# Attention on one core: K's and V's rows dealt four in a row to a partition, in every chunk of every batch

## The chip, the cores and the metric

The kernel runs on one core of one Trainium2 chip. The metric is the device time in microseconds (us) of one execution. Beside the timed runs there is one profiled execution, from which all rows of the profile come.

The core's engines are TensorE (PE, with its weight loads shown apart as PEld), VectorE (DVE), ScalarE (ACT), GpSimd (POOL) and SyncE (SP). Transfers between HBM and SBUF run on 16 DMA engines, whichever engine issued them.

## The reference

Inputs q, k and v have the shape (8, 2048, 512) in fp32; all 8 batches are attended over separately, with one head of width 512.

```python
scores = np.matmul(q, k.transpose(0, 2, 1)) / np.sqrt(d_k)
attn_weights = special.softmax(scores, axis=-1).astype(np.float32)
return np.matmul(attn_weights, v)
```

A sum over the keys does not depend on their order, so any order of a batch's keys gives the same output, if K's rows and V's rows are dealt in the same order. The order of q's rows is that of the output's rows.

## The kernel before

**Layout.** A batch has 2048 rows of q, k and v: 16 blocks of 128 rows (`NKB`), or four chunks of four blocks (`CH = 4`). Rows lie on the 128 partitions. Before the change row n * 128 + p of a batch lies on partition p as block n, for q, k and v alike (`srcs`, from L118).

**Loads.** All loads of fp32 inputs into fp16 tiles are casting DMAs that POOL issues (`load`, L133, for k and q; `load_v`, L221, for v). One load takes a chunk: 128 partitions, four rows of 512 elements each. A row of HBM is 2 KB, and its fp16 copy 1 KB. k and q chunks go to `stage` tiles, of which there are two, shared by both; v goes straight to one of two `vraw` tiles (named vh in the profile), one for odd and one for even batches.

**Transposes.** k and q are needed with the width on the partitions. In batch 0 most of this is done by PE (`first_transpose`, `transposed`), and from batch 1 on by DMA transposes that SP issues (L160), two for each chunk, into `kraw` and `qraw`. POOL may issue a load into a stage tile only when the transposes of the chunk before it in that tile are done, and SP may issue a transpose only when the load has landed. SP also issues every store of the output (L474), in the same queue.

**Matmuls.** Both matrix products are done by Strassen's scheme with seven products of halves in place of eight: sums of blocks are made on DVE (`k_sums` L195 to L198, `q_sums` L212 to L215, `v_sums` L229 to L232, `p_sums` L396 to L399), and a second level of the scheme is used in the product with V (`vi_sums` L267 to L270, `a_sums` L603 to L606, `fine`, whose matmuls are L649). The matmuls of the scores are L343 (`Group.product`) and, for the parts without the scheme, L286 and L302; those of the product with V are L452 (`Pair.product`) and L649. V is the moving operand. Between the products ACT and DVE copy and add PSUM banks (L354 to L368, L664 to L677), ACT does the exponentials (L279), and ACT, DVE and POOL scale and add the output halves (L461, L464, L570; for some the DMA adds them, L565). There are eight tiles for output halves.

**The sum of the weights.** V's second block of a pair has a column of ones next to it, at element 512 of its row, so that one of the matmuls has 257 columns instead of 256 and yields the sum of the weights. POOL writes this column once for each of the two tiles (L855 and L787).

**Order.** The whole order is written out by hand. A batch is four groups of 28 slots; `PRODUCTS`, `SUMS` and `PLAN` say in which slot of which group a product, a sum, a load or a transpose is issued. `PLAN` (L765 to L777) issues the loads and transposes of the next batch. Each engine runs its instructions in that order, and waits where an input is not ready.

**The start.** Batch 0's first row blocks are loaded apart: n = 0 of q by SP and of k by ACT, without a cast (`load_first`, L140), and n = 1 to 3 of q and k by POOL in turn (L833), 128 runs each. Then come k's second chunk in two pieces, the other chunks of q and k, which go into tiles that are free until later (named right and left in the profile), and V. Before the second half of V's load, and before the loads of batch 1, POOL waits at small copies (`gate`, L887, L890, L891).

Of the kernel before, what the change touches and what calls it, by code (L numbers as in the profile page):

```python
# [12 lines left out]
def kernel(  # L13
# [21 lines left out]
    nc = tc.nc  # L35
    P = 128
    B, T, D = q.shape
    F16 = mybir.dt.float16
# [13 lines left out]
    NJ = NKB // 2  # L52
    CH = 4
    NCH = NKB // CH
    H = D // 2
    VP = D + 2
    TP = H + 2
    NG = NJ // 2
    NE = 6
# [9 lines left out]
    const = ctx.enter_context(tc.tile_pool(name="const", bufs=1))  # L69
# [32 lines left out]
    qraw = [const.tile([P, 2 * NT, ND, P], F16, name=f"qraw{n}") for n in range(2)]  # L102
    qsum = [const.tile([P, NT, 2, P], F16, name=f"qs{n}") for n in (1, 2, 4)]

    vraw = [const.tile([P, NJ, 2, VP], F16, name=f"vh{n}") for n in range(2)]
    vt1 = const.tile([P, NJ, TP], F16, name="vt1")
    vt2 = const.tile([P, NJ, H], F16, name="vt2")
    vt4 = const.tile([P, NJ, H], F16, name="vt4")
# [2 lines left out]
    if not ALL:  # L111
# [3 lines left out]
    staged = {}  # L115
    pts = {}

    srcs = {  # L118
        "k": k.rearrange("b (n p) d -> b p n d", p=P),
        "q": q.rearrange("b (n p) d -> b p n d", p=P),  # L120
        "v": v.rearrange("b (n p) d -> b p n d", p=P),
    }

    def load(what, b, c, pieces=(CH,), room=None):
        t = staged.get((what, b, c))
        if room is not None:
            t = staged[what, b, c] = room
        if t is None:
            t = staged[what, b, c] = stage.tile([P, CH, D], F16, tag="stage", name="stage")
        n = CH - sum(pieces)  # L130
        for w in pieces:
            at = c * CH + n
            nc.gpsimd.dma_start(out=t[:, n:n + w, :], in_=srcs[what][b, :, at:at + w, :])  # L133
            n += w

    firsts = {}

    def load_first(what, n, queue, room):
        firsts[what, n] = room
        queue.dma_start(out=room, in_=srcs[what][0, :, n, :])  # L140

    def first_transpose(what, n):

# [12 lines left out]
    def dma_transpose(what, b, c, h):  # L156
        src = staged.pop((what, b, c)) if h else staged[what, b, c]
        dst = raw_of(what, b, c)
        ns = slice(h * CH // 2, (h + 1) * CH // 2)
        nc.sync.dma_start_transpose(  # L160
            out=dst[:, ns].rearrange("p n c r -> p (n c) r"),
            in_=src[:, ns].rearrange("p n d -> p (n d)"),
        )
# [52 lines left out]
        ]  # L216

    def load_v(b, c):
        dst = vraw[b % 2][:].rearrange("p j s d -> p (j s) d")
        ns = slice(c * CH, (c + 1) * CH)  # L220
        nc.gpsimd.dma_start(out=dst[:, ns, 0:D], in_=srcs["v"][b, :, ns, :])  # L221

    def v_sums(b, c=None):
        vh = vraw[b % 2]
        js = slice(0, NJ) if c is None else slice(c * NI, (c + 1) * NI)
        b11, b12 = vh[:, js, 0, 0:H], vh[:, js, 0, H:D]
        b21, b22 = vh[:, js, 1, 0:H], vh[:, js, 1, H:D]
        return [
            lambda: sub(vt1[:, js, 0:H], b12, b11),  # L229
            lambda: sub(vt2[:, js], b22, vt1[:, js, 0:H]),  # L230
            lambda: sub(b12, b22, b12),
            lambda: sub(vt4[:, js], b21, vt2[:, js]),  # L232
        ]

    def vi_blocks(b):
        lo, hi = slice(0, NI), slice(NI, NJ)
        vh = vraw[b % 2][:].rearrange("p j s d -> p s j d")
        return vh[:, :, lo, 0:P], vh[:, :, lo, P:H], vh[:, :, hi, 0:P], vh[:, :, hi, P:H]

    def t3_inner(b, s):  # L240
# [70 lines left out]
    class Group:  # L311
# [6 lines left out]
        def product(self, n):  # L318
            c, j = divmod(self.j, 2)
            a11, a12, a21, a22 = k_blocks(c)  # L320
            b11, b12, b21, b22 = q_blocks(self.sp)
            _, s1, s2, s4 = kops[c]
            t1, t2, t4 = qsum
            t3 = t3_of(self.sp)
            if n == 1:
                if self.sp not in pts:
                    new_p(self.sp)
                self.left, self.right = pts[self.sp][0:2]
                self.x = bank("qx")
# [12 lines left out]
            for dc in range(2):  # L342
                nc.tensor.matmul(  # L343
                    dst[:], lhs[:, j, dc, :], rhs[:, :, dc, :],
                    start=(n in (1, 5) and dc == 0), stop=(dc == 1),
                    skip_group_check=True,
                )
            getattr(self, f"after{n}", lambda: None)()
# [66 lines left out]
    class Pair:  # L415
# [8 lines left out]
        def product(self, n, j0=0, j1=NJ):  # L424
            g = self.g
            left, right = pts[g // 2][0:2]
            s1, s2, s4 = (t[:, :, part(self.which)] for t in psums[g])
            vh, t1, t2, t4 = vraw[g // NQT % 2], vt1, vt2, vt4
            cols = columns(g, self.which)
            alone = g >= NP - 2 and self.which == "b"  # L430
            own = "q" if alone else "p"
            if n == 1 and j0 == 0:
                self.x = bank("px")
            elif n == 2 and type(self) is Pair:
                self.y = bank(own + "y")
            elif n == 5:
                self.z = bank(own + "z")
            lhs, rhs, dst = {
                1: (lambda j: left[0][:, j, cols], lambda j: vh[:, j, 0, 0:H], "x"),
                2: (lambda j: left[1][:, j, cols], lambda j: vh[:, j, 1, 0:width], "y"),  # L440
                3: (lambda j: s4[:, j, :], lambda j: vh[:, j, 1, H:D + 1], "z"),
                4: (lambda j: right[:, j, 1, cols], lambda j: t4[:, j, :], "x"),
                5: (lambda j: s1[:, j, :], lambda j: t1[:, j, 0:H + 1], "z"),
                6: (lambda j: s2[:, j, :], lambda j: t2[:, j, :], "x"),
                7: (lambda j: right[:, j, 0, cols], lambda j: vh[:, j, 0, H:D], "x"),
            }[n]
            dst = getattr(self, dst)
            width = H + 1 if n in (3, 5) or (n == 2 and g == 0) else H
            first = n in (1, 5) or (n == 2 and type(self) is Pair)
            last = n in (2, 3, 4)  # L450
            for j in range(j0, j1):
                nc.tensor.matmul(  # L452
                    dst[:, 0:width], lhs(j), rhs(j),
                    start=(first and j == 0), stop=(j == NJ - 1),
                    skip_group_check=True,
                )
            if j1 == NJ:
                getattr(self, f"after{n}", lambda: None)()
# [325 lines left out]
    def prefetch(g, slot):  # L784
        b, qt = divmod(g, NQT)
        if (g, slot) == (0, 12):
            nc.gpsimd.memset(vraw[1][:, :, 1, D:D + 1], 1.0)  # L787
# [42 lines left out]
        staged[what, 0, 0] = spool.tile([P, CH, D], F16, tag=f"s{n + 1}", name="first")  # L830
    for n in range(1, CH):
        for what in "qk":
            nc.gpsimd.dma_start(out=staged[what, 0, 0][:, n], in_=srcs[what][0, :, n, :])  # L833
    nc.vector.tensor_copy(out=ident[:], in_=ident32[:])
    new_p(0)
    new_p(1)
# [18 lines left out]
    nc.gpsimd.memset(vraw[0][:, :, 1, D:D + 1], 1.0)  # L855
    dummies = {name: bank(name) for name in ("qy", "qz")}

    def idle(n, name="qy", w=512):
# [29 lines left out]
    firsts.pop("v")()  # L888

    nc.gpsimd.tensor_copy(out=gate[:], in_=qraw[1][:, NT - 1, ND - 1, 0:1])  # L890
    nc.gpsimd.tensor_copy(out=gate[:], in_=vraw[0][:, NJ - 1, 1, D - 1:D])  # L891

    def step(n=1):
        for _ in range(min(n, len(background))):
# [22 lines left out]
    for slot in range(14):  # L917
        n, at = divmod(slot, len(QORDER))
        old, what = QORDER[at]
# [23 lines left out]
    for g in range(NP):  # L943
# [4 lines left out]
        for slot in range(NS + 6):  # L948
            n, at = divmod(slot, len(QORDER))
            old, what = QORDER[at]  # L950
# [3 lines left out]
            if slot < NS:  # L954
# [6 lines left out]
                right = prev if at == 2 else None  # L961
# [42 lines left out]
```

## Time and profile before

| | us |
|---|---|
| median of 3 timed runs | 787.62 |
| lowest and highest of them | 787.57, 787.89 |
| the profiled execution | 788.82 |
| span of the profiled execution, first to last instruction | 787.0 |

The granted TensorE clock is 1.000 in the whole span. Busy shares of the span: PE 99%, PEld 68%, DVE 90%, ACT 81%, POOL 15%; the packets of queue 0 (the loads that POOL issues) take 45.0% of the 16 DMA engines' time, those of queue 1 (SP's transposes and stores) 42.1%.

How to read the rows: a group of instructions is named by its line, engine, operation and tiles (out<-in), then come its count, busy time, the mean ns of one, and the idle time of its engine just before it with what ended it. A wait is "who <- what it waited for: total us, times, longest us". In a DMA queue's row stand packets, MB and the share of 16 engines' time. A row of stretches has the length and then the busy time of each engine, with the number of instructions.

### The profile page before, as it was taken

How to read it: one execution, taken by the hardware profiler on the slowest of the kernel's cores; microseconds unless marked ns; L12 is line 12 of the kernel's file. 1: busy time of each engine (PE TensorE's matmuls, PEld its weight loads, DVE VectorE, ACT ScalarE, POOL GpSimd, SP SyncE). 2: the span in 40 equal slices, each digit the busy share in tenths (PEclk: the TensorE clock that was granted, in tenths of full speed). 3: DMA queues.
4: the chain of work that ended last, by engine and by line, in shares of the span. 5: the costliest groups of instructions: out<-in, count | busy, mean ns of one | idle time of the engine just before them, and what ended most of it. 6: DMA issues, size and time to landing. Idle time of an engine off the chain costs nothing.

```text
span 787.0 us, 18104 instructions
## 1 busy us (share of the span) xinstructions
PE 780.7 (99%) x6570; PEld 536.2 (68%) x6570; DVE 711.7 (90%) x1583; ACT 638.4 (81%) x1322; POOL 115.3 (15%) x157
## 2 busy tenths in 40 slices
PE   9999999999999999999999999999999999999998
PEld 6567666666666666666766666676666666666686
DVE  4799999989999899998999989999899998999864
ACT  4688888888888888888888888888888888888852
POOL 5011102012021020211102121021210212100000
PEclk9999999999999999999999999999999999999999
DMA  9999993999839999499976999579993999912122
GB/s 188 170 155 168 172 171 72 193 186 193 163 59 198 147 169 188 89 188 192 185 120 117 186 184 175 110 142 191 168 208 62 160 179 193 192 49 62 47 68 95
DMA packets 210298, 117.13 MB, mean 149 GB/s; under 512 B 126368, under 2 KB 209952, under 8 KB 210208
## 3 DMA queue, kind: packets, MB, share of 16 engines
q0 software_dynamic: 52528, 51.91, 45.0%
q1 hardware_dynamic: 157392, 63.73, 42.1%
q8 instruction: 51, 0.84, 0.4%
q14 instruction: 39, 0.32, 0.1%
q10 hardware_dynamic: 288, 0.33, 0.1%
HBM read 100.73 MB, written 33.55 MB: 171 GB/s over the span
## 4 chain that ended last, share of the span: by engine, by line
PE 94%; DMA 3%; ACT 1%; issue 1%; DVE 1%; POOL 0%; DVEq 0%; ACTq 0%; POOLq 0%
PE t L343 45%; PE t L452 29%; PE t L649 17%; PE t L286 2%; DMA out_dram<-o 2%; PE tr L170 1%; DMA first<-in_q_dram 1%; PE t L302 0%; POOL first L833 0%; ACT o L461 0%; ACT cz L359 0%; POOL o L570 0%; ACT t L354 0%; DVE s L397 0%; ACT left L279 0%
## 5 line engine op out<-in xcount | busy, mean ns | idle before, releaser
L461 ACT ACTIVATE o<-t,r 128x256 f32<-128x256 f32 x300 | 136.7, 478 | 75.8 <-DVE r L487 28.6
L343 PE MATMUL t<-qraw,kraw 128*128 128x512 f16 x728 | 198.1, 379 | 0.1
L279 ACT ACTIVATE left<-t 128x512 f16<-128x512 f32 (+1 forms) x260 | 154.0, 599 | 17.3 <-PE t L343 7.3
L343 PE MATMUL t<-qs,ks 128*128 128x512 f16 x488 | 138.8, 379 | 0.7 <-ACT t L354 0.7
L279 ACT ACTIVATE right<-cz 128x1024 f16<-128x1024 f32 x122 | 129.7, 1063 | 2.3 <-DVE cz L365 2.2
L343 PEld LDWEIGHTS <-kraw 128*128 128x128 f16 x976 | 87.0, 97 | 57.9 <-issue 0.6
L452 PEld LDWEIGHTS <-right 128*128 128x128 f16 x1024 | 99.4, 98 | 37.0 <-DVE right L398 1.4
L452 PEld LDWEIGHTS <-s 128*128 128x128 f16 x1072 | 102.1, 97 | 29.9 <-issue 0.3
L649 PEld LDWEIGHTS <-si 128*128 128x128 f16 x1044 | 76.2, 97 | 36.6
L359 ACT COPY cz<-t 128x512 f32<-128x512 f32 x120 | 70.3, 585 | 35.5 <-PE t L343 34.1
L343 PEld LDWEIGHTS <-ks 128*128 128x128 f16 x732 | 67.9, 97 | 41.4 <-issue 1.4
L368 DVE TENSOR_TENSOR cz<-t,cz 128x512 f32<-128x512 f32 x122 | 83.6, 685 | 11.8 <-ACT o L461 7.0
L464 DVE SCALAR_TENSOR_TENSOR o<-t,r,o 128x256 f32<-128x256 f32 x148 | 69.3, 478 | 19.8 <-ACT ci L667 7.5
L365 DVE TENSOR_TENSOR cz<-t,cz 128x512 f32<-128x512 f32 x122 | 83.3, 683 | 3.8 <-PE t L343 3.3
L649 PEld LDWEIGHTS <-left 128*128 128x128 f16 x928 | 66.1, 97 | 20.7
L354 ACT COPY t<-t 128x512 f32<-128x512 f32 x120 | 69.7, 581 | 4.7 <-PE t L343 1.1
L343 PE MATMUL t<-qraw,ks 128*128 128x512 f16 x244 | 72.5, 378 | 0.2 <-ACT cz L359 0.2
L452 PE MATMUL t<-vt,s 128*128 128x256 f16 (+1 forms) x560 | 72.5, 273 | 0.0
L343 PE MATMUL t<-qs,kraw 128*128 128x512 f16 x244 | 72.5, 379 | 0.0
L362 ACT COPY cz<-t 128x512 f32<-128x512 f32 x122 | 70.9, 581 | 0.4
L649 PE MATMUL t<-vh,left 128*128 128x128 f16 x696 | 67.4, 219 | 0.0
L452 PE MATMUL t<-vh,s 128*128 128x257 f16 x512 | 67.0, 273 | 0.1
(104 smaller groups left out, 1208.0 us busy)
## 6 DMA issues: line engine op xcount, KB each, us to landing
out_dram<-o SPq DMA_DIRECT2D x256, 128.0 KB, 3.7
vh<-in_v_dram POOLq DMA_DIRECT2D x32, 512.0 KB, 9.1
stage<-in_q_dram POOLq DMA_DIRECT2D x28, 512.0 KB, 7.0
stage<-in_k_dram POOLq DMA_DIRECT2D x28, 512.0 KB, 8.2
o<-o POOLq DMA_DIRECT2D x14, 128.0 KB, 2.7
right<-in_q_dram POOLq DMA_DIRECT2D x2, 512.0 KB, 10.5
right<-in_k_dram POOLq DMA_DIRECT2D x2, 512.0 KB, 12.8
qraw<-stage SPq DMA_TRANSPOSE x56, 6.2
```

The source lines that it names most:

```text
L279: nc.scalar.activation(out=out_, in_=in_, func=EXP, scale=inv_sqrt_d)
L286: nc.tensor.matmul(st[:], kops[c][0][:, n, dc, :], qraw[0][:, half * NT:(half + 1) * NT, dc, :], start=(dc == 0), stop=(dc == ND - 1),)
L343: nc.tensor.matmul(dst[:], lhs[:, j, dc, :], rhs[:, :, dc, :], start=(n in (1, 5) and dc == 0), stop=(dc == 1), skip_group_check=True,)
L354: f(out=self.y[:], in_=self.x[:])
L359: f(out=self.cz[:, 1, :], in_=self.z[:])
L362: nc.scalar.copy(out=self.cz[:, 0, :], in_=self.x[:])
L365: nc.vector.tensor_add(self.cz[:, 1, :], self.x[:], self.cz[:, 1, :])
L368: nc.vector.tensor_add(self.cz[:, 0, :], self.z[:], self.cz[:, 0, :])
L452: nc.tensor.matmul(dst[:, 0:width], lhs(j), rhs(j), start=(first and j == 0), stop=(j == NJ - 1), skip_group_check=True,)
L461: nc.scalar.activation(out=out_, in_=src, func=COPY, scale=r[:])
L464: nc.vector.scalar_tensor_tensor(out=out_, in0=src, scalar=r[:], in1=out_, op0=MULT, op1=ADD)
L649: nc.tensor.matmul(dst, lhs[:, j, :], rhs[:, j, :], start=(n == 1 and j == 0), stop=(j == NI - 1), skip_group_check=True,)
```

## The change

The rows of k and v are dealt so that, within each chunk of 512 rows, partition p holds the rows 4 p to 4 p + 3, which are adjacent in HBM. q's rows keep their order, with the chunk as an index of its own. A k load's run grows from one row to four (8 KB read, 4 KB written), where a whole chunk is loaded; k's second chunk in batch 0, loaded in two pieces, gets runs of two rows, and k's first four blocks in batch 0 keep runs of one row, 8 KB apart.

For v, the column of ones had stood after each row (a row took 514 elements, the column filled only for the second of a pair). It now stands after each pair (a pair takes 1026 elements), so that the two rows of a pair are adjacent and a v load's run grows to two rows (4 KB read, 2 KB written). All reads of v are written for the new layout.

```diff
-    VP = D + 2
+    VP = 2 * D + 2
...
-    vraw = [const.tile([P, NJ, 2, VP], F16, name=f"vh{n}") for n in range(2)]
+    vraw = [const.tile([P, NJ, VP], F16, name=f"vh{n}") for n in range(2)]
...
-        "k": k.rearrange("b (n p) d -> b p n d", p=P),
-        "q": q.rearrange("b (n p) d -> b p n d", p=P),
-        "v": v.rearrange("b (n p) d -> b p n d", p=P),
+        "q": q.rearrange("b (c n p) d -> b c p n d", p=P, n=CH),
+        "k": k.rearrange("b (c p n) d -> b c p n d", p=P, n=CH),
+        "v": v.rearrange("b (c p n) d -> b c p n d", p=P, n=CH),
...
-            at = c * CH + n
-            nc.gpsimd.dma_start(out=t[:, n:n + w, :], in_=srcs[what][b, :, at:at + w, :])
+            nc.gpsimd.dma_start(out=t[:, n:n + w, :], in_=srcs[what][b, c][:, n:n + w, :])
...
-        queue.dma_start(out=room, in_=srcs[what][0, :, n, :])
+        queue.dma_start(out=room, in_=srcs[what][0, 0][:, n, :])
...
-        dst = vraw[b % 2][:].rearrange("p j s d -> p (j s) d")
-        ns = slice(c * CH, (c + 1) * CH)
-        nc.gpsimd.dma_start(out=dst[:, ns, 0:D], in_=srcs["v"][b, :, ns, :])
+        js = slice(c * CH // 2, (c + 1) * CH // 2)
+        src = srcs["v"][b, c].rearrange("p (j s) d -> p j (s d)", s=2)
+        nc.gpsimd.dma_start(out=vraw[b % 2][:, js, 0:2 * D], in_=src)
+
+    def v_of(b):
+        return vraw[b % 2][:, :, 0:2 * D].rearrange("p j (s d) -> p j s d", s=2)
+
+    def ones_of(n):
+        return vraw[n][:, :, 2 * D:2 * D + 1]
...
-                1: (lambda j: left[0][:, j, cols], lambda j: vh[:, j, 0, 0:H], "x"),
-                2: (lambda j: left[1][:, j, cols], lambda j: vh[:, j, 1, 0:width], "y"),
-                3: (lambda j: s4[:, j, :], lambda j: vh[:, j, 1, H:D + 1], "z"),
+                1: (lambda j: left[0][:, j, cols], lambda j: vh[:, j, 0:H], "x"),
+                2: (lambda j: left[1][:, j, cols], lambda j: vh[:, j, D:D + width], "y"),
+                3: (lambda j: s4[:, j, :], lambda j: vh[:, j, D + H:2 * D + 1], "z"),
...
-                7: (lambda j: right[:, j, 0, cols], lambda j: vh[:, j, 0, H:D], "x"),
+                7: (lambda j: right[:, j, 0, cols], lambda j: vh[:, j, H:D], "x"),
...
-            nc.gpsimd.dma_start(out=staged[what, 0, 0][:, n], in_=srcs[what][0, :, n, :])
+            nc.gpsimd.dma_start(out=staged[what, 0, 0][:, n], in_=srcs[what][0, 0][:, n, :])
```

`v_sums` and `vi_blocks` read V through `v_of`, the two memsets write the column through `ones_of`, and the last gate reads the last element of V in the new layout; these lines are left out.

More of the change, by code (lines that the diff above doesn't have):

```diff
@@ L218, in load_v @@
     def load_v(b, c):
-        dst = vraw[b % 2][:].rearrange("p j s d -> p (j s) d")
-        ns = slice(c * CH, (c + 1) * CH)
-        nc.gpsimd.dma_start(out=dst[:, ns, 0:D], in_=srcs["v"][b, :, ns, :])
+        js = slice(c * CH // 2, (c + 1) * CH // 2)
[5 more added lines that the diff above has]
+        return vraw[n][:, :, 2 * D:2 * D + 1]
     def v_sums(b, c=None):
-        vh = vraw[b % 2]
+        vh = v_of(b)
         js = slice(0, NJ) if c is None else slice(c * NI, (c + 1) * NI)
@@ L236, in vi_blocks @@
         lo, hi = slice(0, NI), slice(NI, NJ)
-        vh = vraw[b % 2][:].rearrange("p j s d -> p s j d")
+        vh = v_of(b).rearrange("p j s d -> p s j d")
         return vh[:, :, lo, 0:P], vh[:, :, lo, P:H], vh[:, :, hi, 0:P], vh[:, :, hi, P:H]
@@ L786, in prefetch @@
         if (g, slot) == (0, 12):
-            nc.gpsimd.memset(vraw[1][:, :, 1, D:D + 1], 1.0)
+            nc.gpsimd.memset(ones_of(1), 1.0)
         for kind, what, c, *h in PLAN.get((qt, slot), ()):
@@ L854 @@
     nc.gpsimd.memset(ui[1][:, :, P:P + 1], 1.0)
-    nc.gpsimd.memset(vraw[0][:, :, 1, D:D + 1], 1.0)
+    nc.gpsimd.memset(ones_of(0), 1.0)
     dummies = {name: bank(name) for name in ("qy", "qz")}
@@ L890 @@
     nc.gpsimd.tensor_copy(out=gate[:], in_=qraw[1][:, NT - 1, ND - 1, 0:1])
-    nc.gpsimd.tensor_copy(out=gate[:], in_=vraw[0][:, NJ - 1, 1, D - 1:D])
+    nc.gpsimd.tensor_copy(out=gate[:], in_=vraw[0][:, NJ - 1, 2 * D - 1:2 * D])
     def step(n=1):
```

## The prediction

> **What bounds the kernel now.** I read the busy line of the page first, then the stretches of the span, then the chain of waits at the start and round the one gap in the middle, then the waits of the engines and of the SP queue, and the DMA views last.
>
> ```profile
> PE 780.7 (99%) x6570; PEld 536.2 (68%) x6570; DVE 711.7 (90%) x1583; ACT 638.4 (81%) x1322; POOL 115.3 (15%) x157
> ...
> 0.00:24.00 24.00, 22.37 (x168) 14.44 (x169) 11.16 (x24) 11.87 (x22) 10.43 (x22) 1.00 1.10 191
> 24.00:287.00 263.00, 262.59 (x2166) 176.56 (x2165) 246.52 (x543) 219.05 (x448) 39.34 (x54) 1.00 0.97 156
> 287.00:300.00 13.00, 12.42 (x108) 8.42 (x106) 11.08 (x29) 10.42 (x24) 2.22 (x3) 1.00 1.26 198
> 300.00:768.00 468.00, 468.00 (x4004) 323.80 (x4002) 434.89 (x974) 392.37 (x820) 63.30 (x78) 1.00 0.83 144
> 768.00:787.04 19.04, 15.29 (x136) 12.96 (x134) 8.04 (x16) 4.73 (x10) 0.00 (x0) 1.00 0.28 92
> ```
>
> The stretch rows give the length, then the busy time of PE, PEld, DVE, ACT and POOL, the granted clock, the DMA share and GB/s. From 300 to 768 us PE has no idle time at all (468.00 of 468.00) while the DMA engines carry 0.83. The whole budget of PE idle time is 24.00 - 22.37 = 1.63 us at the start, 0.41 up to 287, 0.58 in the 13 us after it, none to 768, and 19.04 - 15.29 = 3.75 at the end: 6.4 us. A busy PE in this view is not PE at its peak, but a load can only shorten time in which PE waits for it, so this budget is the most that faster loads could touch.
>
> Who waits for a transfer?
>
> ```profile
> POOL stage L133 <- DMA qraw<-stage: 186.0, 14, 16.3
> ...
> POOL gate L891 <- DMA vh<-in_v_dram: 6.8, 1, 6.8
> ...
> ACT o L461 <- DMA out_dram<-o: 1.2, 2, 0.9
> ...
> DVE ks L195 <- DMA kraw<-stage: 1.1, 1, 1.1
> ...
> PEld L170 <- DMA first<-in_q_dram: 0.4, 1, 0.4
> ...
> SPq L160 <- DMA stage<-in_q_dram: 68.2, 14, 19.8
> ...
> SPq L160 <- DMA stage<-in_k_dram: 3.3, 2, 2.9
> ```
>
> Columns: total us, times, longest. The large waits belong to POOL (it waits for a stage buffer before it may issue the next load) and to SP (it waits for a q load before it may transpose it). Neither reaches PE: ACT, DVE and PE wait for stores, transposes and first rows for 1.2 + 1.1 + 0.4 = 2.7 us in the whole run, and none of them waits for a V load; POOL's gate at the start does, for 6.8 us, and holds only the loads of the next batch.
>
> **The change part by part.**
>
> *The K and V loads in steady state (32 chunks each).* A chunk goes on moving 1 MB of fp32 into 512 KB of fp16; its runs grow from 2 KB to 8 KB (K) and 4 KB (V), so 512 runs become 128 and 256.
>
> ```profile
> DMA packets 2464, 2.46 MB, mean 205 GB/s; under 512 B 78, under 2 KB 2463, under 8 KB 2463
> ...
> q0 software_dynamic: 2463, 2.44, 123.1%
> ...
> q0 software_dynamic: 52528, 51.91, 45.0%
> ...
> q8 instruction: 51, 0.84, 0.4%
> ...
> vh<-in_v_dram POOLq DMA_DIRECT2D x32, 512.0 KB, 9.1
> ...
> stage<-in_k_dram POOLq DMA_DIRECT2D x28, 512.0 KB, 8.2
> ```
>
> The first two rows are from the stretch 12 to 24 us, where nearly only casting loads run. They land 205 GB/s of fp16, which is 410 GB/s of fp32 read, and a packet occupies its engine for 1.231 x 16 x 12 us / 2463 = 96 ns. A chunk of 1 MB therefore takes 1.05 MB / 410 GB/s = 2.6 us of pure transfer; the 8 to 9 us to landing are the issue, other traffic and the receipt. What would a packet of 8 KB read cost? No row shows one that casts. At the low end it costs less than four packets of 2 KB (4 x 96 = 384 ns) by whatever is fixed in a packet; were a quarter of the 96 ns fixed (an estimate), 4 KB packets would save an eighth and 8 KB packets 19%, 0.5 us of K's 2.6. At the high end stand the instruction fetches (16 KB each, 0.84 MB in 51): 0.4% x 16 x 787 us / 51 = 988 ns, 62 ns per KB where a 2 KB casting packet takes 48, so 29% more, +0.8 us a K chunk. I take a few per cent less, nearest to the casting rows. Either end is hidden: k transposes made DVE wait once (1.1 us) and V never, and PE stood still for none of it in the 468 us. Cost: 0.0. If the cover were gone, 28 later K chunks at +0.8 us could cost up to 22 us, but it would need each of them to be late already, and one in 28 is.
>
> *POOL's issue.*
>
> ```profile
> L221 POOL DMA_DIRECT2D vh<-in_v_dram x32 | 26.1, 815 | 0.8 <-PE t L649 0.5 <-DMA stage<-in_k_dram 0.3
> ...
> L133 POOL DMA_DIRECT2D stage<-in_k_dram x30 | 24.4, 815 | 103.9 <-DMA qraw<-stage 77.3 <-DMA kraw<-stage 14.7 <-ACT left L279 11.2
> ...
> L833 POOL DMA_DIRECT2D first<-in_k_dram x3 | 1.7, 575 | 0.0
> ```
>
> A load of 512 runs holds POOL 815 ns, one of 128 runs 575. So K's loads issue up to 0.24 us faster and V's by some 0.16 (256 runs, in between). POOL is busy 15% and waits 104 us ahead of these K issues alone; the saving is waiting in another place: 0.0.
>
> *V's new layout.* The tile changes from rows of 514 to pairs of 1026 elements; matmuls still stream 256 or 257 adjacent elements, and the sums keep their shapes.
>
> ```profile
> L229 DVE TENSOR_TENSOR vt<-vh x16: 671/679/685, 37.2 to 696.6; 128x1024 f16<-128x1024 f16 x16
> ...
> L232 DVE TENSOR_TENSOR vt<-vh,vt x16: 677/686/1022, 46.7 to 730.4; 128x1024 f16<-128x1024 f16 x16
> ...
> L213 DVE TENSOR_TENSOR qs<-qraw,qs 128x1024 f16<-128x1024 f16 x16 | 11.6, 725 | 0.1
> ...
> L452 PE MATMUL t<-vh,s 128*128 128x257 f16 x512 | 67.0, 273 | 0.1
> L452 PE MATMUL t<-vt,s 128*128 128x256 f16 x512 | 66.3, 273 | 0.0
> ```
>
> V's sums at an odd pitch (median 679 to 686 ns) take what Q's sums of the same size in an even layout take (725 mean), and the matmuls on vh and on vt are equal at 273. Pitch has no price in these rows, either way: 0.0.
>
> *The start.* K's first rows are now every fourth row of the chunk: 2 KB runs as before, 8 KB apart in HBM. q's order is unchanged.
>
> ```profile
> 1.25 2.29 POOL first L833 x4
> 3.54 5.07 DMA first<-in_q_dram
> 8.65 0.40 PE tr L170 x4
> ...
> 6.00:8.00 2.00, 1.76 (x22) 1.58 (x20) 1.15 (x3) 0.43 (x1) 2.00 (x4) 1.00 1.23 185
> 8.00:10.00 2.00, 1.80 (x25) 1.47 (x23) 1.14 (x4) 0.66 (x2) 2.00 (x4) 1.00 1.17 178
> ```
>
> The chain of waits: four small loads are issued, the fifth (q, n=3) lands 5.07 us after its own issue, and from 8.65 on the chain is PE. Before it in the same queue stand q and k for n=1 and n=2, all of 2 KB runs then as now. I take 0.0. Above, K's scattered rows could read slower (a rival below); below, if the larger runs behind them left these loads alone sooner, the 0.24 + 0.20 = 0.44 us that PE idles in 6 to 10 us is all there is.
>
> *The one gap in the middle.*
>
> ```profile
> 276.59 0.74 POOL L133 DMA_DIRECT2D stage<-in_k_dram  x1 [11.17 <-ACT left L279]
> ...
> 278.71 0.78 POOL L221 DMA_DIRECT2D vh<-in_v_dram  x1
> ...
> 278.80 12.35 DMA out_dram<-o
> ...
> 291.18 0.47 ACT L461 ACTIVATE o<-t,r 128x256 f32<-128x256 f32 x1 [0.91 <-DMA out_dram<-o]
> ...
> out_dram<-o SPq DMA_DIRECT2D x256, 128.0 KB, 3.7
> ```
>
> A store that usually lands in 3.7 us took 12.35 among a K and a V load issued beside it; ACT had no free output half, came 0.91 us late, and PE lost the 0.58 us of the stretch 287 to 300. Both loads beside it are of the changed kind. If they leave the engines a little earlier, this gap shrinks; it may as well turn up in another batch. I count half of it: -0.3 us (ends -0.58 and +0.58).
>
> **Sum:** 0 + 0 + 0 + 0 - 0.3 = -0.3 us. The profiled execution took 788.82 us with a span of 787.0 (1.8 outside it); its own time after would be 788.5. The three timed runs have the median 787.62, 1.2 below the profiled one; the difference carries over: **787.3 us**. A measurement of this kernel can tell about 0.2% (1.6 us) from no change, so the forecast is no change.
>
> **The rivals.**
>
> *Long packets hold up the stores: slower.* The SP queue's stores share the 16 engines with POOL's loads. If an engine finishes a packet before it turns to another queue, each of a store's 128 / 16 = 8 packets per engine can wait for a K packet of 384 ns where it waited for 96: 8 x 288 ns = 2.3 us more, 6.0 instead of 3.7. It reaches PE through the eight output halves: ACT's o L461 waits, and its next bank copy comes late. For it: the 12.35 us store shows the path and the price, 0.58 us. Against it: only 2 of 300 halves waited at all (1.2 us), and the longer packets are fewer, so loads as a whole hold the engines no longer. It decides from three such gaps on (1.7 us); once in each of the seven batches that prefetch gives 7 x 0.58 = 4.1 us, 791.7; I put the case at 789.4 (three). The Trainium skill, DMA: Bandwidth & Descriptors, section "Queues, rings and completion order", says that an engine takes its queue rows in turn and drains a whole packet before it switches, which is this rival's premise; no run here shows the order of packets, and its section on SWDGE also prefers packets of up to 4096 B, by which four 1 KB rows could have been one turn already and nothing would change.
>
> *K's scattered first rows: later start.* If reading 2 KB out of every 8 KB ran at half the rate, each of the two k loads ahead of q n=3 (256 KB read, 0.64 us at 410 GB/s) would add 0.64 us, with the k rows n=0 on the other queue 1.9 us in all. PE follows from 8.65 on: 788.9 to 789.5. For it: the path is bare there. Against it: runs of 2 KB reach 410 GB/s already, though of adjacent rows.
>
> *More of the idle time goes: faster.* All 0.99 us of the middle and the 0.44 of the start: 786.2. For it: the gap at 291 us and the wait at 8.65 are both the wake of a transfer.
>
> ```profile
> PE t L343 <- ACT t L354: 0.7, 2, 0.4
> ```
>
> Against it: this is PE's largest wait for another engine after the start, for a bank copy of ACT, and only one of its two cases lies in the wake of the late store.
>
> *The runs are cut up again,* and the engines see 2 KB packets: 787.6.
>
> **How the numbers follow.** Forecast (hidden, 786.9 to 788.2) 0.62; stores late 0.13, all slower; scattered rows 0.08, half of it slower; more idle time gone 0.09, of which 0.04 passes -0.2%; runs cut up 0.08, same. Faster 0.04, slower 0.17, same 0.79. The range runs from 786.2 (every idle microsecond that a load could touch) to 789.5 (three late stores, or the scattered rows at full price); beyond it lie the batches with a late store each, about 1 in 10.
>
> **What would show it.** In the page after: packets of queue 0 down from 52528 to about 32,600 (52528 less 30 x 384 and 256 for K and 32 x 256 for V), POOL's K issues near 575 ns, queue 0's share between 38% and 55%; PE again 468.00 of 468.00 late in the span; no new wait of ACT for out_dram. The prediction is wrong if PE idles in the steady stretch, if q n=3 lands later than about 9 us, or if matmuls or sums on vh change their duration, for which I know no reason.

## The result, and the profile after

| | before | after |
|---|---|---|
| median of 18 runs each, us | 787.75 | 788.95 |
| lowest and highest | 787.36, 788.24 | 788.36, 792.41 |
| the profiled execution, us | 788.82 | 788.91 |
| its span, us | 787.0 | 787.1 |

The ratio after to before is 1.0022, with a 95% interval of 1.0015 to 1.003: the change makes the kernel slower by 1.2 us, where the forecast was 787.3 us, 0.3 less than before. Not only the median moved. All 18 runs before lie within 0.9 us; of the 18 after, six are over 790 and the longest is 792.41.

The two profiled executions differ by 0.09 us only, and it would be easy to read "no change" from them. The one of before, with 788.82, is longer than each of its 18 timed runs. The two lost their time in different places, as the stretches show. First the page of the changed kernel, the lines that answer to those of before: busy time, the queue of POOL's loads, then the DMA issues with their median time to landing.

```profile
PE 780.0 (99%) x6570; PEld 534.8 (68%) x6570; DVE 711.9 (90%) x1583; ACT 639.0 (81%) x1322; POOL 107.3 (14%) x157
...
q0 software_dynamic: 32560, 51.91, 42.0%
...
out_dram<-o SPq DMA_DIRECT2D x256, 128.0 KB, 3.6
vh<-in_v_dram POOLq DMA_DIRECT2D x32, 512.0 KB, 8.7
...
stage<-in_k_dram POOLq DMA_DIRECT2D x28, 512.0 KB, 7.5
```

The change does what it says: 52528 packets became 32560 for the same 51.91 MB, their share of the engines fell from 45.0% to 42.0%, and a K chunk lands in 7.5 us instead of 8.2, a V chunk in 8.7 instead of 9.1. POOL issues both faster, K in 595 ns instead of 815 and V in 733; the groups of POOL in the changed kernel:

```profile
L220 POOL DMA_DIRECT2D vh<-in_v_dram x32 | 23.4, 733 | 0.6 <-DMA stage<-in_k_dram 0.5
L132 POOL DMA_DIRECT2D stage<-in_k_dram x30 | 17.8, 595 | 120.6 <-DMA qraw<-stage 77.1 <-DMA kraw<-stage 33.5 <-issue 9.8
```

POOL is busy 8 us less (115.3 to 107.3), and waits 17 us longer ahead of these very issues (103.9 to 120.6): the saving went into a wait. Now the stretches of the changed kernel, with the same columns as before (length, then busy time of PE, PEld, DVE, ACT, POOL, the granted clock, DMA share, GB/s):

```profile
0.00:24.00 24.00, 20.78 (x160) 12.77 (x161) 11.29 (x24) 10.83 (x21) 9.63 (x22) 1.00 1.03 185
24.00:287.00 263.00, 262.88 (x2159) 176.31 (x2157) 245.23 (x541) 219.19 (x448) 36.20 (x54) 1.00 0.92 159
287.00:300.00 13.00, 13.00 (x120) 9.06 (x118) 12.09 (x32) 11.42 (x26) 2.22 (x3) 1.00 1.14 202
300.00:768.00 468.00, 468.00 (x4006) 323.68 (x4004) 435.19 (x974) 392.80 (x820) 59.25 (x78) 1.00 0.78 142
768.00:787.10 19.10, 15.34 (x137) 13.01 (x134) 8.11 (x16) 4.74 (x10) 0.00 (x0) 1.00 0.27 93
```

PE's idle time is now 3.22 us at the start (1.63 before), 0.12 up to 287 (0.41), none in the next 13 us (0.58), none to 768, 3.76 at the end (3.75). From 300 to 768 us nothing has changed: 468.00 of 468.00. The start lost 1.59 us; the gap in the middle isn't there in this execution.

What did PE wait for at the start? Its timeline in the changed kernel (start, us, engine, line, operation, and in brackets the idle time before it with what ended it), the three rows with a wait:

```profile
5.51 0.66 PE L145 MATMUL tr<-ident,cz 128*128 128x128 f32 x4 [0.69 <-DMA cz<-in_k_dram]
...
7.43 0.40 PE L169 MATMUL tr<-ident,first 128*128 128x128 f16 x4 [0.82 <-DMA first<-in_k_dram]
...
10.78 0.40 PE L169 MATMUL tr<-ident,first 128*128 128x128 f16 x4 [0.47 <-DMA first<-in_k_dram]
```

Each waits for K rows, n = 0, n = 1 and n = 3, and none for q. The waits sum to 1.98 us. In the DMA view of the first 9 us the loads that PE waits for stand like this before:

```profile
first<-in_q_dram POOLq DMA_DIRECT2D x3, 128.0 KB, 3.8
first<-in_k_dram POOLq DMA_DIRECT2D x3, 128.0 KB, 3.9
...
cz<-in_k_dram ACTq DMA_DIRECT2D x1, 256.0 KB, 3.3
```

and like this after:

```profile
first<-in_q_dram POOLq DMA_DIRECT2D x3, 128.0 KB, 5.5
first<-in_k_dram POOLq DMA_DIRECT2D x3, 128.0 KB, 5.7
...
cz<-in_k_dram ACTq DMA_DIRECT2D x1, 256.0 KB, 4.3
```

K's first rows take 1.8 us longer to land from POOL's queue and 1.0 us from ACT's. q's rows, which are read as before, take 1.7 us longer as well. Two of their three loads stand behind loads of K in the same queue. The first, q n = 1, does not, and it lands in 4.9 us instead of 3.8 too; beside it runs K's n = 0, which ACT issued just before; whether that is what delays it is not shown.

A single row tells how late the whole kernel is from there on: the first and the last sum on V. After:

```profile
L234 DVE TENSOR_TENSOR vt<-vh x16: 671/679/686, 38.6 to 696.7; 128x1024 f16<-128x1024 f16 x16
```

Before it ran from 37.2 to 696.6. The changed kernel is 1.4 us late at 38 us, and then needs 658.1 us from the first sum to the last, where the profiled execution of before needed 659.4. So that one lost 1.3 us on the way, in which its timed runs seem not to share: 788.82 less 1.3 is 787.5, near their median of 787.75. In what follows this row's first time is the measure of the start.

### The profile page after: what moved, and what is told of

Same layout as the page of the kernel before. It is cut to its first block, busy times and chain, and to the rows that moved or that the text cites. A ratio compares the mean times of both kernels' runs of the same rounds, so it can differ in the third digit from the quotient of the medians.

```text
span 787.1 us, 18104 instructions
## 1 busy us (share of the span) xinstructions
PE 780.0 (99%) x6570; PEld 534.8 (68%) x6570; DVE 711.9 (90%) x1583; ACT 639.0 (81%) x1322; POOL 107.3 (14%) x157
## 3 DMA queue, kind: packets, MB, share of 16 engines
q0 software_dynamic: 32560, 51.91, 42.0%
## 4 chain that ended last, share of the span: by engine, by line
PE 97%; DMA 1%; ACT 1%; DVE 0%; POOL 0%; issue 0%; DVEq 0%; ACTq 0%; POOLq 0%
PE t L348 47%; PE t L457 30%; PE t L654 17%; PE t L291 2%; DMA first<-in_k_dram 1%; PE tr L169 1%; POOL first L838 0%; PE t L307 0%; DVE s L402 0%; ACT o L466 0%; DVE s L404 0%; ACT right L284 0%; ACT t L359 0%; ACT cz L364 0%; ACT left L284 0%
## 6 DMA issues: line engine op xcount, KB each, us to landing
right<-in_k_dram POOLq DMA_DIRECT2D x2, 512.0 KB, 12.4
```

## The experiments

**The theory after the result:** all of the loss is batch 0's start, where K's first four blocks are read 2 KB out of every 8 KB (chunk 1's two pieces 4 KB out of every 8). **The rivals:** the long runs cost something in the later batches too (stores, transposes); V's new layout; or the longer loads that stand behind the first ones at the start. In the short diffs, a `-` line is the changed kernel's unless it is said otherwise. A run of the kernel before stood beside each group of experiments; its medians were 787.66 to 787.86.

**Chunk 0 of batch 0 in the old order.**

```diff
+    def src_of(what, b, c):
+        if what != "q" and (b, c) == (0, 0):
+            x = (k if what == "k" else v)[0, 0:CH * P]
+            return x.rearrange("(n p) d -> p n d", p=P)
+        return srcs[what][b, c]
...
-        queue.dma_start(out=room, in_=srcs[what][0, 0][:, n, :])
+        queue.dma_start(out=room, in_=src_of(what, 0, 0)[:, n, :])
```

> The changed kernel, with batch 0's first chunk of K and V alone in the old order (its first loads of K read adjacent rows again); V's part of it is loaded in two halves. Theory A (K's scattered first rows land late and PE starts late, and the long runs do nothing else): the start is as before, PE idles about 1.6 us less in the first 24 us than in the changed kernel, and the time is that of the kernel before, 787.3 to 787.9, with its narrow spread. Theory B (the long packets of the steady state hold up stores and transposes): as the changed kernel, 788.6 to 789.2, with its wide spread.

Measured: 788.09 us (787.46 to 791.7, 12 runs), ratio to before 1.0008 [0.9998, 1.0019]. Ten of the twelve runs are at or below 788.64. About 0.9 of the 1.2 us comes back when 512 of 16384 rows of K and V are dealt as before and all the rest stays as changed. The profiled execution was the longest of the twelve, 791.7, and it isn't the start that makes it so (first V sum at 37.7 us):

```profile
24.00:768.00 744.00, 741.88 (x6247) 507.06 (x6246) 690.23 (x1540) 621.86 (x1290) 97.87 (x136) 1.00 0.86 148
```

2.1 us of PE idle time fell into the middle here. The chain of waits there has a store that took 14.78 us to land, and ACT waiting for it:

```profile
182.83 14.78 DMA out_dram<-o
...
197.63 0.47 ACT L477 ACTIVATE o<-t,r 128x256 f32<-128x256 f32 x1 [2.28 <-DMA out_dram<-o]
```

It was issued beside a V load at 182.75 us, and PE waited 2.0 us for ACT's next bank copy. This is the scene of the prediction's rival "long packets hold up the stores"; the profile of the kernel before has it too, with short packets and a store of 12.35 us. Runs this long are few (two of the twelve here, one of 790.54 among 31 of the kernel before), and one of them must not be taken for the effect of an edit.

**The other way round: the kernel before, with chunk 0 of batch 0 alone dealt four in a row** (one-row runs, as the start has them).

```diff
+        if what != "q" and (b, c) == (0, 0):
+            return (k if what == "k" else v)[0, 0:CH * P].rearrange("(p n) d -> p n d", p=P)
...
-        queue.dma_start(out=room, in_=srcs[what][0, :, n, :])
+        queue.dma_start(out=room, in_=src_of(what, 0, 0)[:, n, :])
```

(Here `-` is the kernel before.)

> The kernel before, with only batch 0's first chunk of K and V dealt four rows in a row to a partition; every run stays one row of 2 KB. Theory A: all of the loss, 788.6 to 789.3, with the wide spread of the changed kernel, and q's and k's first blocks land 1 to 2 us later. Theory B: no loss, 787.5 to 788.0.

Measured: 790.0 us (788.22 to 790.64, 7 runs), ratio 1.0023 [1.0012, 1.0035]. There isn't one long run in this kernel, V has its old layout, and all of the loss is there, even more than the forecast 788.6 to 789.3. So the loss needs neither long loads nor V's new layout. K's first rows land in 5.7 us, as in the changed kernel. It shows something more. The stretches of its start:

```profile
4.00:6.00 2.00, 1.67 (x12) 1.02 (x12) 0.76 (x2) 0.56 (x1) 2.00 (x5) 1.00 1.04 137
6.00:7.40 1.40, 0.00 (x0) 0.00 (x0) 0.35 (x1) 0.02 (x1) 0.82 (x2) 1.00 1.14 174
7.40:10.80 3.40, 3.37 (x24) 2.87 (x25) 1.01 (x3) 0.59 (x2) 3.13 (x5) 0.51 1.17 177
```

PE stands still until k n = 1 lands, and then the granted clock is 0.51 for 3.4 us: the wait is paid, and then the matmuls behind it run at half speed. The Trainium skill, TensorE: Matmul & The Clock Gate, section "Part 1: The HAM clock gate", tells of a gate that halves the clock after an idle window of about 3.4 us. The value and the length of the spell agree here. How long PE must idle for it is less clear, as the rows ahead of the spell show:

```profile
2.44 1.49 PE L864 MATMUL t<-warm 128*128 128x512 f16 x3
3.96 1.43 PE L150 MATMUL tr<-ident,cz 128*128 128x128 f32 x8
5.49 0.40 PE L174 MATMUL tr<-ident,first 128*128 128x128 f16 x4
7.43 0.61 PE L174 MATMUL tr<-ident,first 128*128 128x128 f16 x4 [1.54 <-DMA first<-in_k_dram]
```

PE waited for 1.54 us in one piece. But all of its 1.67 us of work from 4 to 6 us are transposes: from the end of the dummy matmuls with which the kernel starts, at 3.93, to the first product at 7.83 it did nothing else, for 3.9 us. In the profile of the changed kernel, at full clock throughout, the longest wait is 0.82 us and the stretch without anything but transposes 3.7 us (3.93 to 7.67). Which of the two the clock answers to is not shown here.

**Two pitches in between and beyond.** First, chunk 0 of batch 0 dealt in pairs, 2 KB of every 4 KB:

```diff
+            return x.rearrange("(m p r) d -> m p r d", p=P, r=2)
...
+            pairs = v[0, 0:CH * P].rearrange("(m p r) d -> p m (r d)", p=P, r=2)
```

> The changed kernel, with batch 0's first chunk of K and V dealt in pairs: K's first loads read 2 KB out of every 4 KB instead of every 8 KB. Theory A with a cost that grows with the pitch: half of the loss, 788.0 to 788.5. Theory A with a cost of any scattered reading: all of the loss, 788.6 to 789.2. Theory B: 788.6 to 789.2 too, but with no late landing in the first 10 us.

Measured: 788.17 us (787.45 to 789.79, 12 runs), ratio 1.0004 [0.9995, 1.0012]. K's first rows land in 4.6 us. Most of the loss is gone.

Then sixteen rows in a row to a partition, over the whole of each batch: the later loads keep runs of 8 KB and 4 KB, and K's first rows are 2 KB out of every 32 KB.

```diff
-        "k": k.rearrange("b (c p n) d -> b c p n d", p=P, n=CH),
-        "v": v.rearrange("b (c p n) d -> b c p n d", p=P, n=CH),
+        "k": k.rearrange("b (p c n) d -> b c p n d", p=P, n=CH),
+        "v": v.rearrange("b (p c n) d -> b c p n d", p=P, n=CH),
```

> The changed kernel, with all of K and V dealt sixteen rows in a row to a partition over the whole batch: the runs stay 8 KB and 4 KB, but a chunk's runs lie 32 KB apart, and K's first loads read 2 KB out of every 32 KB. Theory A with a cost that grows with the pitch: the first blocks land still later, 790 or more. Theory A with a cost of any scattered reading: 788.6 to 789.3. Theory B: as the changed kernel, unless the loads of 8 KB runs slow down when these are not adjacent; then DVE waits for K's transposes.

Measured: 787.61 us (787.08 to 788.49, 11 runs), ratio 0.9994 [0.9985, 1.0003]. All of the loss is gone, though the rows lie farther apart than ever, which none of the three cases had expected. "Scattered rows are slow" is therefore too simple: what counts is how far apart.

**Chunks 0 and 1 of batch 0 in the old order,** to see whether chunk 1's pieces hold what the first experiment had left over.

```diff
+        if what != "q" and b == 0 and c < 2:
+            x = (k if what == "k" else v)[0, c * CH * P:(c + 1) * CH * P]
+            return x.rearrange("(n p) d -> p n d", p=P)
```

> The changed kernel, with the first two chunks of K and V of batch 0 in the old order (chunk 1's two loads of k read adjacent rows again too). Theory A, now for both chunks (a load that takes 2 or 4 KB out of every 8 KB is slow, and the long runs elsewhere are worth nothing): the start of the kernel before, 787.4 to 787.9. Rival C (the changed steady state costs something too): over 788.2. Rival D (the long runs are a gain that the start hid): under 787.2.

Measured: 788.28 us (786.91 to 789.24, 11 runs), ratio 1.0005 [0.9996, 1.0014]. It missed: it should have come to 787.4 to 787.9. By the number rival C came true (over 788.2), but in the profile PE idles for only 0.11 us from 24 to 768 us, and the last experiment below speaks against C. The interval holds no change as well as the 0.3 to 0.6 us that these two experiments show against the kernel before. What the old order of the start leaves when the rest is changed isn't settled by these two.

**Sixteen KB:** eight rows in a row to a partition, over half a batch.

```diff
+        "k": k.rearrange("b (h p r n) d -> b h r p n d", p=P, r=2, n=CH),
+        "v": v.rearrange("b (h p r n) d -> b h r p n d", p=P, r=2, n=CH),
...
+        return srcs[what][b, c] if what == "q" else srcs[what][b, c // 2, c % 2]
```

> The changed kernel, with K and V dealt eight rows in a row to a partition over half a batch: first loads of k read 2 KB out of every 16 KB, chunk 1 4 KB out of every 16 KB; all other runs stay 8 and 4 KB. If the pitch of 8 KB alone is bad: as with 32 KB, 787.4 to 787.9. If the cost falls steadily from 8 to 32 KB: 788.0 to 788.5. If the cost had to do with the distance of the runs in general: at least 788.9.

Measured: 788.12 us (787.66 to 789.74, 11 runs), ratio 1.0007 [0.9998, 1.0016]; K's first rows land in 5.7 us at the median, as at 8 KB, but n = 0 in 3.6 us instead of 4.3. It lies between 8 and 32 KB.

**Blocks 1 to 3 of K's chunk 0 in one load,** so that 6 KB out of every 8 KB are read at once; chunk 1 as before the change.

```diff
+        if n == 1:
+            nc.gpsimd.dma_start(out=staged["k", 0, 0][:, 1:CH], in_=srcs["k"][0, 0][:, 1:CH, :])
```

> The changed kernel, with k's blocks 1 to 3 of the first chunk in one load of 6 KB runs 8 KB apart (128 runs instead of 384), and only chunk 1 of batch 0 in the old order. If it is the reading in small parts at this pitch that is slow: the start is as before or better, 787.4 to 787.9. If any reading at a pitch of 8 KB is slow: 788.5 or more, and k's blocks land at 8 us or later.

Measured: 790.64 us (790.37 to 791.07, 5 runs), ratio 1.0037 [1.0025, 1.005]. It's the slowest of all, and every run shows a mean granted clock of 0.998 or 0.999. The load of three blocks lands after 6.33 us, at 8.30, where three single loads bring n = 1 at 7.38 in the changed kernel; the longer wait ends in half the clock again:

```profile
6.00:8.00 2.00, 0.71 (x7) 0.30 (x5) 0.42 (x1) 0.58 (x1) 1.05 (x2) 0.98 1.05 173
8.00:10.00 2.00, 1.66 (x12) 1.41 (x13) 0.42 (x1) 0.00 (x0) 1.31 (x3) 0.50 1.20 194
```

Three times the data took 0.6 us longer to land than one block's median 5.7 (6.33): the three single loads of the changed kernel had all landed only at 10.8. By the expectation the second case came true (over 788.5, and landing after 8 us); yet the load is three times as large, and there is no such load of adjacent rows to compare it with, so this run does not tell size from distance. It does show that PE needs the first block early, not three blocks soon.

**Seven more idle matmuls at the start of the changed kernel,** ahead of the transposes that wait for K (the kernel has such fillers at other places already), to part the waits from the clock.

```diff
+    idle(2)
     first_transpose("k", 0)
+    idle(2)
...
+    idle(2)
     transposed("k", 0, 1, 1, dve, "pz")
...
+    idle(1)
     transposed("k", 0, 3, 1, dve, "pz")
```

> The changed kernel with seven more dummy matmuls of 512 columns at the start, ahead of the transposes of k's blocks 0, 1 and 3, where PE waited. Theory E (the runs far above the median are those in which PE idles so long at the start that its clock stays or falls to half for some us): the median stays near 789, or a few tenths above, and no run is over 789.8. If the spread comes from transfers alone: a third of the runs are still over 789.8.

Measured: 789.17 us (788.46 to 790.12, 11 runs), ratio 1.002 [1.0011, 1.0029]. The median doesn't come down, as it can't if the landing times set it. The longest runs are shorter than those of the changed kernel (790.12 against 792.41), but three of eleven are still above 789.8, nearly the third of them that the other case had. None of the eleven has a mean clock below 0.999, so half clock is not what makes these three long.

**Six KB:** block 0 of chunk 0 is 128 adjacent rows, blocks 1 to 3 are 2 KB of every 6 KB.

```diff
+        if n == 0:
+            return k[0, 0:P]
+        return k[0, P:CH * P].rearrange("(p n) d -> p n d", p=P)[:, n - 1, :]
```

> The changed kernel with another deal of batch 0's first chunk: block 0 of K and V are 128 adjacent rows, and blocks 1 to 3 read 2 KB out of every 6 KB (V's part comes in three loads). Theory A2 (first loads at a pitch of 8 KB, or near it, land late; the load of block 0 by ACT's queue holds up the others): blocks land between the cases of 4 and 8 KB, 788.1 to 788.7. If the first load of block 0 alone did the harm: the start as before, 787.5 to 788.2. If any distance between 4 and 16 KB costs the same: 788.7 or more.

Measured: 788.24 us (787.64 to 795.4, 12 runs), ratio 1.0011 [0.9995, 1.0026], of which one run of 795.4 makes the interval wide. K's first rows land in 4.1 us at the median, nearest to the 3.9 of before and not between the cases of 4 and 8 KB; but the last of them, n = 3, takes 5.8 us, and PE waits 0.75 us for it. The time is in the forecast range, the landing is not.

**The kernel of the second experiment with six idle matmuls ahead of k n = 1,** where its PE had stood still.

```diff
+    idle(6)
     transposed("k", 0, 1, 1, dve, "pz")
```

> The kernel before with batch 0's first chunk alone dealt four in a row (790.0 without more), and six dummy matmuls of 512 columns more, where PE waited 1.5 us for k's block 1. Theory E (a wait of PE of this length at the start lets its clock fall to half for 3.4 us, which costs some 1.3 us beside the wait): 788.4 to 789.0, and no stretch at half clock in the first 20 us. If the late rows alone make the 790: 789.8 or more.

Measured: 789.05 us (788.67 to 790.8, 9 runs), ratio 1.002 [1.0011, 1.0029]. The same stretches as above, without the half clock:

```profile
6.00:7.40 1.40, 1.35 (x11) 0.73 (x10) 0.42 (x1) 0.58 (x1) 0.82 (x2) 1.00 1.13 176
7.40:10.80 3.40, 3.34 (x38) 2.31 (x37) 1.70 (x4) 0.66 (x2) 2.62 (x4) 1.00 1.24 203
```

38 matmuls instead of 24 in the same 3.4 us. K's first rows land no earlier (6.2 us at the median). So of the 2.2 us that the second experiment had lost by the medians, the fillers take away about 1, and 1.2 to 1.3 are left, as much as the whole change loses at its median. That the 1 us is the clock alone is not shown: three of the seven runs of the second experiment have a mean clock of 1.0, and two of these took 789.78 and 789.92.

**Thirty-two KB once more,** the same kernel as above, since its gain over the change carries the argument.

```diff
+        "k": k.rearrange("b (p c n) d -> b c p n d", p=P, n=CH),
+        "v": v.rearrange("b (p c n) d -> b c p n d", p=P, n=CH),
```

> Sixteen rows in a row to a partition over the whole batch, once more and on one chip with the run beside it. If the long runs are worth nothing and 32 KB apart costs nothing at the start: 787.5 to 787.9, the kernel before within 0.1%. If the first measurement was luck: 788.0 or more.

Measured: 787.66 us (787.35 to 788.77, 11 runs), ratio 1.0001 [0.9992, 1.0009]. It stands: no loss, and no gain on the kernel before.

**Batch 0 alone at 32 KB; batches 1 to 7 as the change has them.**

```diff
+        if what != "q" and b == 0:
+            x = (k if what == "k" else v)[0]
+            return x.rearrange("(p c n) d -> c p n d", p=P, n=CH)[c]
+        return srcs[what][b, c]
```

> The changed kernel with batch 0 alone dealt sixteen rows in a row to a partition; batches 1 to 7 keep the change's deal, four rows in a row in each chunk. Theory A2 (all of the loss comes from batch 0's start): as the run beside it, 787.5 to 787.9. Theory B (the change's loads in the later batches cost something too, through stores or transposes): 788.2 or more, with PE idle after 24 us.

Measured: 787.61 us (787.3 to 788.0, 11 runs), ratio 0.9997 [0.9988, 1.0006]. This is the experiment that settles it. Seven of eight batches are the changed kernel's, to the byte of every load; the median is 1.3 us below it, and none of the 11 runs is above 788.0. Its loads at the start:

```profile
first<-in_k_dram POOLq DMA_DIRECT2D x3, 128.0 KB, 4.7
cz<-in_k_dram ACTq DMA_DIRECT2D x1, 256.0 KB, 3.2
```

and its first stretches after the start, beside the sums on V:

```profile
4.00:8.00 4.00, 3.58 (x31) 2.88 (x31) 1.94 (x4) 0.59 (x1) 3.61 (x7) 1.00 1.21 182
8.00:12.00 4.00, 4.00 (x48) 3.38 (x46) 1.84 (x6) 1.87 (x6) 3.06 (x8) 1.00 1.10 175
...
300.00:768.00 468.00, 468.00 (x4009) 324.20 (x4007) 434.36 (x972) 392.09 (x819) 59.28 (x78) 1.00 0.77 141
```

```profile
L240 DVE TENSOR_TENSOR vt<-vh x16: 669/680/692, 37.1 to 695.1; 128x1024 f16<-128x1024 f16 x16
```

The same two stretches of the changed kernel:

```profile
4.00:8.00 4.00, 2.44 (x20) 1.59 (x18) 1.25 (x3) 0.59 (x1) 2.80 (x6) 1.00 1.13 160
8.00:12.00 4.00, 3.53 (x41) 2.72 (x39) 1.99 (x5) 0.66 (x2) 2.96 (x5) 1.00 1.11 170
```

PE has 7.58 us of work in the 8 us from 4 to 12, where the changed kernel has 5.97: 1.6 us more. The first V sum comes at 37.1 instead of 38.6, and from it to the last takes 658.0 us (658.1 in the changed kernel). The two profiled executions are 787.3 and 788.91, 1.6 apart. The late V sum, the missing work at the start and the time of the execution agree, and nothing is left for the other batches.

The other profiled executions say the same. The time of each, less that of its first V sum, is 750.2 to 750.5 us in nine of the fourteen kernels here, the changed one (750.3) and this one (750.2) among them. It is 750.7 and 750.8 in the two with fillers, and larger only in the second experiment (751.2), the kernel before (751.6) and the first experiment with its late store (754.0). What sets the slower deals apart has happened by the first V sum, at 37 to 40 us.

No version here beats the kernel before: the best two deals come to 0.9994 to 1.0001 of it, with no change inside each interval.

## Why the prediction was wrong

**The steady K and V loads: right.** They were costed at 0.0 either way because PE has no idle time from 300 to 768 us for a load to touch. They got faster (42.0% of the engines' time, inside the forecast 38% to 55%; mean packet time 0.420 x 16 x 787.1 us / 32560 = 162 ns, where the 108 ns of before are 0.450 x 16 x 787.0 / 52528), and the last experiment, with seven batches of them, stands at 0.9997 of before.

**POOL's issue and V's layout: right.** The K issue came to 595 ns (575 forecast). V's came to 733, a saving of 0.08 us where 0.16 was forecast. POOL spends the difference waiting. V's sums take 679 ns at the median, as before.

**"The start ... I take 0.0": this step failed.** It put the landing of K's first rows at no change because their runs stay at 2 KB, and left their distance out of the sum. The budget of PE's idle time, from which the prediction starts, bounds a gain and says nothing of a loss. The rival "K's scattered first rows", given 0.08, was the right one, and nearly in size: it had 1.9 us at the loads and 788.9 to 789.5 for the time; the loads came 1.0 us (n = 0) and 1.8 us (n = 1 to 3) later, PE lost 1.6, and the time is 788.95, inside the stated range, whose upper end this rival had set with the late stores. It put the place a little wrong: it had q n = 3 as the row that PE would miss. q n = 3 did land late, 9.3 us into the span (5.8 us after its issue) so past the "about 9 us" that the prediction had named as a sign against itself. But PE missed three of K's own blocks, from 5.51 us on, so the evidence "PE follows from 8.65 on" was from the end of a path that can break at each of its four blocks. The argument against it ("runs of 2 KB reach 410 GB/s already, though of adjacent rows") named its own weakness and then was weighed as if it had none.

**"I count half of it: -0.3" for the gap in the middle, and "the difference carries over": this failed too.** The profiled execution of before was 1.2 us above the median of its runs, and PE's idle time from 24 to 768 us, 0.99 us where the changed kernel has 0.12, is most of that; 0.58 of it is the gap. A gap that the median run doesn't have can't be gained there, and that the median run lacks it is what the times suggest, as no run near the median was profiled. Without this term, and with the 1.4 us by which the first V sum is late, the sum would have been 787.62 + 1.4 = 789.0.

**The rival "long packets hold up the stores": not the cause of this loss, but not ruled out as a risk.** Stores land in 3.6 us at the median (3.7 before) and in 9.9 at most (12.4 before), PE's stretch from 300 to 768 us is full, and the changed kernel's waits have no ACT waiting for a store. But the first experiment, a kernel with the long loads, met a store of 14.78 us that stopped PE for 2.0 us, and the kernel before met one of 12.35 us with short packets. How often either kernel meets one can't be told from single profiles. The rival's premise, which the prediction took from the Trainium skill (DMA: Bandwidth & Descriptors, section "Queues, rings and completion order"), that an engine drains a whole packet before it switches, is tested by none of these runs.

**A small misreading.** The 2.7 us of waits for transfers leave out two rows of the same list, 0.8 us of weight loads waiting for the identity matrix and 0.2 us of PE for q's first rows. Neither changes the forecast.

**What stays open.** Every one of these deals moves V's rows of the chunk along with K's, so V's part isn't tested alone; in the profile of the changed kernel only POOL's gate waits for V, as before. Why 8 KB is the worst distance isn't shown; only the landing times are. Of the six runs of the changed kernel over 790 us, four have a mean granted clock of 1.0, the longest two (791.41 and 792.41) among them; the other two, and one of 789.65, have 0.997 to 0.998. So half clock may explain some of the long runs and not the longest, of which there is no profile; a late store like that of the first experiment could make one, and that is not shown. None of the 33 runs with batch 0 dealt at 32 KB is above 788.8. How a late start would bring the long runs is open. Nor is it settled why the two kernels with the old order in batch 0's first chunks stay at 788.1 to 788.3; their K n = 2 landed in 4.8 and 4.5 us where the kernel before has 3.9, though the rows are adjacent.

## What to carry to other kernels

Deal the first loads of a kernel, which nothing hides, apart from the steady ones: a layout that makes long runs for whole chunks makes scattered short ones for the pieces that the start loads singly. Idle time of an engine bounds what faster loads can win, and it bounds no loss; a bare path wants a price for the loss of its own. And ahead of costing a gap seen in one profiled execution, compare that execution with the median of the runs: what it has and they have not can't be won.

## What the hardware showed that was not expected

The distance between 2 KB reads matters, and not in one direction. Time to landing of K's block n = 1, the first of them in POOL's queue, the median of n = 1 to 3, and the time of the whole kernel:

| one block's rows lie apart by | n = 1, us | median of n = 1 to 3, us | kernel, us |
|---|---|---|---|
| 2 KB (the kernel before) | 3.7 | 3.9 | 787.75 |
| 2 KB (chunk 0 old; chunks 0 and 1 old) | 3.9; 4.0 | 4.8; 4.5 | 788.09; 788.28 |
| 4 KB | 4.3 | 4.6 | 788.17 |
| 6 KB (n = 0 adjacent) | 3.8 | 4.1 | 788.24 |
| 8 KB (the change; chunk 0 alone) | 5.4; 5.4 | 5.7; 5.7 | 788.95; 790.0 |
| 16 KB | 4.9 | 5.7 | 788.12 |
| 32 KB (both full versions; batch 0 alone) | 4.5, 4.7; 4.5 | 4.7, 5.0; 4.7 | 787.61, 787.66; 787.61 |

Each landing is from one execution, with other traffic beside it. Adjacent rows alone give medians from 3.9 to 4.8, so the medians up to 5.0 can't be told apart. What stands out is n = 1 at 8 KB: 5.4 us, and 5.9 and 6.0 in the two kernels with fillers, against 3.7 to 4.0 for adjacent rows. The kernel's time follows these landings only roughly: 32 KB lands later than adjacent rows and costs nothing. The Trainium skill, DMA: Bandwidth & Descriptors, section "Latency and other measured facts", reports lower rates at row distances of large powers of two: 207 GB/s at 512 KiB, 164 at 2 MiB and 103 at 4 and 8 MiB, where 214 is full. No run here has such a distance; in these runs 8 KB is the slowest, and 32 KB, four times as far, much less so.

The other surprise is how little waiting can stand ahead of a spell at half clock: 1.54 us of it at the start, in 3.9 us with nothing else but transposes, was followed by 3.4 us at 0.51. With six dummy matmuls in that wait the spell was gone, and the median 1 us lower.
